# Interleaving the heads on TensorE: the recurrent scan, the first half's attention scores, and attention values on two column halves

## Chip, cores and metric

One core of a Trainium2 chip. The metric is the device time of one execution in microseconds (us); the time of a kernel is the median of its runs. Engines: PE (TensorE, matrix products), DVE (VectorE), ACT (ScalarE), POOL (GpSimd), SP (SyncE, which here only issues DMA transfers). PE's products are written to PSUM, from which DVE and ACT read.

## What is computed

One encoder layer over 1024 tokens of width 1024, in float32. A projection `x @ W_in` feeds two branches, which are merged; two layer norms and a product-key mixture of experts (PEER) follow. What matters here are the two branches.

```python
# branch A: forgetting attention, 8 heads of 64, causal, 128-query blocks
s = einsum('bhqd,bhkd->bhqk', q, k) * scale + c[q] - c[k]     # c: cumulative log forget gate
p = softmax(where(causal, s, -inf))
out = einsum('bhqk,bhkd->bhqd', p, v)

# branch B: RWKV-7, 8 heads of 64, a state of 64x64 per head
def frame_step(state, inp):
    sa = einsum('bhij,bhj->bhi', state, -kk_t)
    state = state * w_t + sa[..., None] * (kk_t * a_t) + v_t[..., None] * k_t
    return state, einsum('bhij,bhj->bhi', state, r_t)
...
x = LayerNorm(alpha * x + (sig(gA) * (yA @ P_A) + sig(gB) * (yB @ P_B)) @ W_o)
x = LayerNorm(alpha * x + PEER(x))     # 8 heads, top 16 of 16384 experts per token
```

## The kernel before

**Stages.** The tokens go in two halves of 512. Each half runs `fox` (branch A), `rwkv_half` (branch B), `merge_half` and `queries` (the expert scores). Then a dense block computes the experts of token tiles 5 to 7 over all 16384 experts, while the experts of tiles 0 to 4 are gathered row by row.

**Order of the work.** PE's order in the halves is the order in which the program is written; DVE, ACT and POOL get their queues from the framework's planner. Two things are woven into PE's order. A `Filler` holds projections of the next step; `F.fill(us)` issues as many of them as make up so much estimated time (`fill` in `fox`, `wait(WT[..])` in `rwkv_half`). A `Background` holds the top-k selection and the gathered experts (`topk`, `experts_in`): every `mm` and every transpose ticks it with the product's estimated time, and it issues its next piece when it has credit. The background has something to do only once the first half's expert scores exist, so in the second half and the dense block. It is mostly DVE work (top-k, and a reduction of 128x1024 for each gathered set of rows) and gathers on POOL's DMA queue. All this counts matmuls by their shapes, not by their time on the chip.

**Attention (`fox`).** The loop goes over `ct`, four pairs of heads; head `e` of a pair has its 64 features on partitions 64e to 64e+63 (`r`). For each block of 128 queries (`qi`) the scores against up to 512 keys are five products into the tile `S`: three with the high and low parts of q and k (`qh kh`, `qh kl`, `ql kh`, 64 rows of the array), one that adds the forget bias (`csel`, `ck`, 128 rows) and, on the last block of keys, the causal mask. In the first half (`joint`, four key tiles) both heads of a pair share one `S` tile of two banks, head 1 from column 512 on; in the second half the heads go one after the other. DVE takes the row maximum (`nm`), ACT the exponential (`pr`). The probabilities are transposed and multiplied with the values in `chunks`, a generator in the list `tail` that is advanced by `step` between later score blocks: per key block `kb` it transposes into `pt`, copies on ACT to `th`, and `pv` multiplies the 64 value columns `vc` with `th` into `po`, rows `r` of the output. `pv` runs one key block behind. At the end ACT copies `po` to `yu`, and after the second head `yu` is scaled by the reciprocal row sums and stored. The constant `PV32` is (1,1), so the branch with split values, and its DRAM tensor `vd`, is never taken.

**Scan (`unit` in `rwkv_half`).** Each pair of heads has eight chunks of 64 tokens. After the intra-chunk products (`M`, the triangular levels, `W_`, `At`, `Q`) a loop over the chunks carries the state `sigma`: per chunk and head two products make the next state (`BK` with `AV` over 128 rows, `At` with the state over the head's 64 rows), a copy by DVE (even chunks) or ACT (odd chunks) puts it into SBUF, and two products give the output (`AV` with `M`, the state with `Q`). Each head writes its own 64 partitions of the same PSUM tiles. A float32 product is two records in the trace.

Of the kernel before, what the change touches and what calls it, by code (L numbers as in the profile page):

```python
# [10 lines left out]
F32 = mybir.dt.float32  # L11
F32R = mybir.dt.float32r
# [8 lines left out]
T = 1024  # L21
# [31 lines left out]
SBUFS = 2  # L53
ORD, YTX = 1, 1
LNA = 1
PV32 = (1,1)
SM = 45
MANUAL = {mybir.EngineType.PE}
ALL = {mybir.EngineType.PE, mybir.EngineType.Pool, mybir.EngineType.DVE}
# [305 lines left out]
def body(ctx, g):  # L365
# [13 lines left out]

    g.yfd = dram("yfd", (512, T))  # L380
    g.kd = dram("kd", (4, 2, 128, T))
    g.vd = dram("vd", (T, 1024))
    g.vfd = dram("vfd", (T, 512))
    g.bvd = dram("bvd", (512, T))
    g.gtd = [dram(f"gtd{p}", (16, 128, n)) for p, (_, n) in enumerate(PARTS)]
# [125 lines left out]
def fox(g, hf, X):  # L511
# [2 lines left out]
    t0, n = g.t0, g.n  # L514
    nq, nb, ntt = n // 128, t0 // 128, (t0 + n) // 128
    joint = ntt <= 4
    f32 = PV32[hf]
    ck = g.ck
    cols = g.cols
    with ExitStack() as fx:  # L520
# [30 lines left out]
        with tc.tile_pool(name="fg", bufs=1) as fg, tc.tile_pool(name="xr", bufs=2) as xr:  # L551

            z = fg.tile([8, n], F32, name="z")
            ps = psA.tile([128, n], F32, name="pj")
            run(proj_gen(g, ps, FOX_F, X, 0))
            act.activation(z, ps[0:8, :], AF.Identity, bias=g.vec[0:8, V_FB:V_FB + 1])
            na = fg.tile([8, n], F32, name="na")
            dve.scalar_tensor_tensor(na, z, -1.0, z, op0=OP.mult, op1=OP.min)
            e = fg.tile([8, n], F32, name="fe")
            act.activation(e, na, AF.Exp)  # L560
            u = na
            dve.tensor_scalar(u, e, 1.0, None, op0=OP.add)
            lu = fg.tile([8, n], F32, name="flu")
            act.activation(lu, u, AF.Ln)
            dve.scalar_tensor_tensor(u, u, -1.0, e, op0=OP.add, op1=OP.subtract)
            dve.tensor_sub(lu, lu, u)
            dve.scalar_tensor_tensor(lu, z, 0.0, lu, op0=OP.min, op1=OP.subtract)
            dve.memset(e, 1.0)
            cc = z
            dve.tensor_tensor_scan(cc, e, lu, g.ccar, op0=OP.mult, op1=OP.add)  # L570
            dve.tensor_copy(g.ccar, cc[:, n - 1:n])
            act.activation(ck[0:8, cols], cc, AF.Copy, scale=-1.0)
            dve.scalar_tensor_tensor(ck[32:40, cols], cc, -1.0, ck[0:8, cols].bitcast(F32), op0=OP.mult, op1=OP.subtract)
            if "c" in g.dbg:
                sp.dma_start(g.dbg["c"][:, cols], cc)
            vw = fg.tile([128, 2, 4, 1024], F32R, name="vw")
            for c in range(4):
                raw = xr.tile([128, 1024], F32, name="xraw")
                sp.dma_start(raw, A["w"][FOX_V + c])
                split(g, vw[:, 0, c, :], vw[:, 1, c, :], raw, pool if c % 2 else dve)  # L580
            raw = xr.tile([128, 1024], F32, name="xraw")
            sp.dma_start(raw, A["foxtab"][:, 0:1024])
            act.copy(csel, raw.rearrange("p (a b) -> p a b", a=8))
            raw = xr.tile([128, 1024], F32, name="xraw")
            sp.dma_start(raw[:, 0:128], A["foxtab"][:, 1024:1152])
            act.copy(caus, raw[:, 0:128])
            act.copy(identr, ident)
            run(qk(0, psA))

            for tt in range(nq):  # L590
                ps = psA.tile([128, 512], F32, name="pj")
                t = slice(tt * 128, (tt + 1) * 128)
                for k in range(8):
                    s = slice(k * 128, (k + 1) * 128)
                    mm3(g, ps, X[0][:, k, t], X[1][:, k, t], vw[:, 0, :, s], vw[:, 1, :, s], k == 0, k == 7)
                rows_ = slice(t0 + tt * 128, t0 + (tt + 1) * 128)
                if any(PV32[hf:]):
                    vf = xr.tile([128, 512], F32, name="vf")
                    act.copy(vf, ps)
                    act.dma_start(g.vfd[rows_, :], vf)  # L600
                if all(PV32[hf:]):
                    continue
                vhl = xr.tile([128, 8, 2, 64], F32R, name="vhl")
                split(g, vhl[:, :, 0, :], vhl[:, :, 1, :], ps.rearrange("p (h d) -> p h d", h=8))
                act.dma_start(g.vd[rows_, :], vhl.rearrange("p h a d -> p (h a d)").bitcast(F32))
        fg2.close()
        vp = fx.enter_context(tc.tile_pool(name="vp", bufs=1))
        psS = fx.enter_context(tc.tile_pool(name="psS", bufs=2, space=PSUM))
# [16 lines left out]
        def chunks(ct, e, P_, yu, su, vc):  # L625
# [2 lines left out]
            pend = []  # L628
            r, x = (slice(0, 64), slice(64, 128)) if e == 0 else (slice(64, 128), slice(0, 64))

            def pv(kb, o, th, tl):
                vv = vc[:, kb, :]
                if f32:
                    mm(g, po[r, o:], vv, th[:, o:], kb == 0, kb == ntt - 1)
                    return
                mm(g, po[:, o:], vv, th[:, o:], kb == 0, False)
                mm(g, po[:, o:], vv, tl[:, o:], False, kb == ntt - 1)

            for kb in range(ntt):
                q0 = max(0, kb - nb)  # L640
                pt = psT.tile([128, n], F32, name="pt")
                for qi in range(q0, nq):
                    pe.transpose(pt[:, qi * 128:(qi + 1) * 128], P_[qi][:, kb * 128:(kb + 1) * 128], ident)
                    g.B.tick(0.11)
                o = q0 * 128
                th = sm.tile([128, n], F32 if f32 else F32R, name="th")
                tl = None
                if f32:
                    act.copy(th[:, o:], pt[:, o:])
                else:  # L650
                    tl = sm.tile([128, n], F32R, name="tl")
                    split(g, th[:, o:], tl[:, o:], pt[:, o:])
                pend.append((kb, o, th, tl))
                if len(pend) > 1:
                    pv(*pend.pop(0))
                yield
            for p_ in pend:
                pv(*p_)
            if f32:
                act.copy(yu[r, :], po[r, :])  # L660
            else:
                yt = sm.tile([128, n], F32, name="yt", bufs=1)
                act.copy(yt[r, :], po[x, :])
                dve.tensor_add(yu[r, :], po[r, :], yt[r, :])
            yield
            if e:
                dve.reciprocal(su, su)
# [13 lines left out]
        for ct in range(4):  # L681
# [1 line left out]
            (qh, ql), (kh, kl) = qkt["q", ct], qkt["k", ct]  # L683
            vcs = []
            for h in (2 * ct, 2 * ct + 1):
                if f32:
                    vc = vp.tile([128, ntt, 64], F32, name="vc", bufs=24 // ntt)
                    sp.dma_start(vc, g.vfd[0:ntt * 128, h * 64:(h + 1) * 64].rearrange("(t p) c -> p t c", p=128))
                    vcs.append(vc)
                    continue  # L690
                vc = vp.tile([128, ntt, 128], F32R, name="vc", bufs=24 // ntt)
                sp.dma_start(vc.bitcast(F32), g.vd[0:ntt * 128, h * 128:(h + 1) * 128].rearrange("(t p) c -> p t c", p=128))
                vcs.append(vc)
            if ct < 3:
                F.add(qk(ct + 1, psJ), f"qk{ct + 1}")
# [2 lines left out]
            for es in ((0, 1),) if joint else ((0,), (1,)):  # L698
                P_ = {e: [] for e in es}
                for qi in range(nq):  # L700
                    q = slice(qi * 128, (qi + 1) * 128)
                    nk = (nb + qi + 1) * 128
                    ps = psS.tile([128, T], F32, name="S")
                    for e in es:
                        h = 2 * ct + e
                        r = slice(64 * e, 64 * e + 64)
                        base = 512 * e if joint else 0
                        for b0 in range(0, nk, 512):
                            b1 = min(nk, b0 + 512)
                            ks = slice(b0, b1)  # L710
                            o = ps[:, base + b0:base + b1]
                            mm(g, o, qh[r, q], kh[r, ks], True, False)
                            mm(g, o, qh[r, q], kl[r, ks], False, False)
                            mm(g, o, ql[r, q], kh[r, ks], False, False)
                            last = b1 == nk
                            mm(g, o, csel[:, h, :], ck[:, ks], False, not last)
                            if last:
                                mm(g, ps[:, base + nk - 128:base + nk], identr, caus, False, True)
                            step(1)
                            F.fill(fill)  # L720
# [20 lines left out]
def rwkv_half(g, hf, X, kt):  # L741
# [12 lines left out]
    with ExitStack() as fx:  # L754
# [164 lines left out]
        def unit(ct):  # L919
# [101 lines left out]
            for c in range(NC):  # L1021
                par = c % 2
                pss = psS.tile([128, 64], F32, name="s")
                for e in range(2):
                    r = rows[e]
                    mm(g, pss[r, :], BK[:, e, c, :], AV[:, e, c, :], True, False)
                    mm(g, pss[r, :], At[r, c, :], g.sigma[r, ct, par, :], False, True)
                (act.copy if c % 2 or SM & 64 else dve.tensor_copy)(g.sigma[:, ct, 1 - par, :], pss)
                for e in range(2):
                    r = rows[e]  # L1030
                    mm(g, py[r, c, :], AV[:, e, c, :], M[:, e, c, 0:64], True, False)
                    mm(g, py[r, c, :], g.sigma[r, ct, par, :], Q[r, c, :], False, True)
                wait(WT[7])
            act.copy(yr[:, ct, :], fl(py))
# [806 lines left out]
```

## Time and profile before

| | |
|---|---|
| time, median of 3 runs (lowest, highest) | 3988.88 us (3987.24, 3991.28) |
| the profiled execution, its time and its span | 3954.7 us, 3952.9 us |
| busy share of the span: PE, DVE, ACT, POOL | 85%, 58%, 31%, 59% |
| mean granted clock of TensorE | 0.897 |
| attention of the first half, of the second half | 62 to 201 us, 890 to 1130 us |
| recurrent branch of the first half, of the second half | 201 to 640 us, 1130 to 1690 us |
| dense loop | from 2530 us to the end |

A row of the timeline has the start and the length in us, the engine, the line of the kernel, the operation, the written and the read tile, the rows and columns of the array, the shape of the moving data, and the number of records merged into it. Most products have line 263, that of the helper `mm`, so the tile's name tells them apart. A merged row's length reaches from the first start to the last modelled end, and the ends of pipelined products overlap; the cost of a product is read from the distance between starts. In the scan's rows `Tm` is the buffer that holds `At`, `x` the one that holds `Q`, and `s` stands for both PSUM tiles (`pss` and `py`).

### The profile page before, as it was taken

The numbers are of one execution on the slowest core, as the hardware profiler recorded it, in microseconds if no ns is written. First come the engines' busy times: TensorE is split into PE (matmuls) and PEld (weight loads), VectorE is DVE, ScalarE is ACT, GpSimd is POOL, SyncE is SP. The second block draws the span as 40 slices with busy tenths as digits, with TensorE's granted clock in tenths as the row PEclk, the third lists the DMA queues.
The fourth block names the chain that finished last, engine by engine and source line by source line (L and its number), as shares of the span: only waits on it lengthen the run. The fifth ranks groups of instructions, "written<-read, shape, count | busy, mean of one in ns | idle before, by whom it ended". The sixth has DMA issues, their size and how long they took to land. (4 is left out here: it accounts for less than half of the span.)

```text
span 3952.9 us, 55417 instructions
## 1 busy us (share of the span) xinstructions
PE 3367.2 (85%) x20656; PEld 2429.7 (61%) x20656; DVE 2310.8 (58%) x4773; ACT 1243.7 (31%) x2522; POOL 2341.8 (59%) x1848
## 2 busy tenths in 40 slices
PE   7999999989987877877837676699998899999998
PEld 5577676775555655656713333477776677776676
DVE  3133423448889887899637576366665576733334
ACT  3342212333333111122214343233333333333333
POOL 2031114435666546667647667688887788777872
PEclk9898898998988777888968778799999899999999
DMA  4121114447777666877768789999998999999993
GB/s 134 43 91 36 36 63 138 168 150 243 259 256 260 213 213 223 292 252 262 278 250 269 263 289 301 322 362 367 375 349 319 374 377 387 376 367 406 403 407 128
DMA packets 376575, 1018.03 MB, mean 258 GB/s; under 512 B 108273, under 2 KB 124913, under 8 KB 376049
## 3 DMA queue, kind: packets, MB, share of 16 engines
q0 software_dynamic: 184320, 671.17, 46.5%
q1 hardware_dynamic: 179872, 322.54, 23.9%
q10 hardware_dynamic: 12112, 20.78, 1.4%
q8 instruction: 162, 2.65, 0.3%
q14 instruction: 109, 0.88, 0.1%
HBM read 960.03 MB, written 54.33 MB: 257 GB/s over the span
## 5 line engine op out<-in xcount | busy, mean ns | idle before, releaser
L1398 POOL DMA_INDIRECT g<-u,eidx x640 | 779.0, 1217 | 436.5 <-DVE hh L1403 154.6
L1403 DVE CUSTOM_DVE_ANT_0 g<-g,ext 128x1024 f32<-128x1024 f32 x640 | 879.5, 1382 | 230.3 <-DMA g<-u,eidx 228.7
L281 POOL TENSOR_TENSOR wl<-wraw,wh 128x1024 fp32r<-128x1024 f32 x131 | 322.9, 2465 | 562.4 <-ACT wh L280 513.1
L1675 POOL DMA_INDIRECT vr<-v,ve x454 | 488.6, 1076 | 130.3 <-issue 104.1
L263 PE MATMUL pg<-vr,win 128*32 128x512 f32 x1816 | 307.8, 645 | 115.6 <-DMA vr<-v,ve 115.3
L263 PE MATMUL b<-xh,uh 128*128 128x384 f32 x1024 | 353.7, 345 | 52.2 <-DVE C L1561 29.6
L263 PE MATMUL b<-xh,ul 128*128 128x384 f32 x1024 | 357.4, 349 | 19.1 <-POOL ul L281 19.1
L263 PE MATMUL b<-xl,uh 128*128 128x384 f32 x1024 | 351.9, 344 | 0.0
L263 PE MATMUL v<-vl,ch 128*128 128x512 f32 x768 | 310.1, 404 | 22.7 <-POOL vl L281 22.6
L263 PE MATMUL pj<-xh,wh 128*128 128x512 f32 x624 | 292.0, 468 | 22.3 <-DVE ql L546 8.5
L280 ACT CAST wh<-wraw 128x1024 fp32r<-128x1024 f32 x150 | 157.2, 1048 | 486.3 <-PE pj L263 264.3
L263 PE MATMUL v<-vh,cl 128*128 128x512 f32 x768 | 305.3, 398 | 0.0
L263 PE MATMUL v<-vh,ch 128*128 128x512 f32 x768 | 304.7, 397 | 0.0
L280 ACT CAST uh<-uraw 128x512 fp32r<-128x512 f32 x256 | 158.7, 620 | 399.4 <-PE b L263 359.0
L263 PE MATMUL pj<-xh,wl 128*128 128x512 f32 x624 | 262.0, 420 | 6.4 <-POOL wl L281 3.7
L263 PE MATMUL pj<-xl,wh 128*128 128x512 f32 x624 | 263.9, 423 | 1.9 <-DVE xl L281 1.9
L1675 POOL DMA_INDIRECT C<-v,ve x186 | 196.6, 1057 | 105.3 <-issue 39.4
L263 PEld LDWEIGHTS b<-xh,uh 128*128 128x128 f32 x1024 | 196.7, 192 | 66.5 <-DVE C L1561 34.3
L263 PEld LDWEIGHTS b<-xh,ul 128*128 128x128 f32 x1024 | 196.6, 192 | 56.6 <-issue 32.7
L281 POOL TENSOR_TENSOR ul<-uraw,uh 128x512 fp32r<-128x512 f32 x128 | 170.6, 1333 | 92.8 <-ACT uh L280 66.7
L281 DVE TENSOR_TENSOR vl<-vraw,vh 128x512 fp32r<-128x512 f32 x128 | 122.8, 960 | 171.4 <-ACT vh L280 164.7
L263 PEld LDWEIGHTS pg<-vr,win 128*32 128x32 f32 x1816 | 52.3, 112 | 275.2 <-DMA vr<-v,ve 191.4
(352 smaller groups left out, 6897.9 us busy)
## 6 DMA issues: line engine op xcount, KB each, us to landing
wraw<-w SPq DMA_DIRECT2D x150, 512.0 KB, 3.5
uraw<-ut SPq DMA_DIRECT2D x128, 512.0 KB, 6.9
vraw<-vt SPq DMA_DIRECT2D x128, 512.0 KB, 6.7
cd<-S SPq DMA_DIRECT2D x30, 512.0 KB, 15.6
C<-cd SPq DMA_DIRECT2D x80, 192.0 KB, 6.1
g<-u,eidx POOLq DMA_INDIRECT x640, 6.1
gtd<-tmp ACTq DMA_DIRECT2D x32, 256.0 KB, 3.1
g<-gtd SPq DMA_DIRECT2D x32, 256.0 KB, 3.3
```

The source lines that it names most:

```text
L263: g.pe.matmul(o, l, r, start=start, stop=stop_)
L280: g.act.copy(hi, src)
L281: (lo_eng or g.dve).tensor_sub(lo, src, hi.bitcast(F32))
L1398: pool.indirect_dma_start(out=gg, out_offset=None, in_=A["u"], in_offset=bass.IndirectOffsetOnAxis(ap=idx[:, s_:s_ + 1], axis=0))
L1403: dve.tensor_tensor_reduce(out=gg, in0=gg, in1=xt, scale=1.0, scalar=0.0, op0=OP.mult, op1=OP.add, accum_out=hh[:, k:k + 1])
L1675: g.pool.indirect_dma_start(out=place, out_offset=None, in_=g.A["v"], in_offset=bass.IndirectOffsetOnAxis(ap=self.meta[i][1][:, t:t + 1], ...
```

## The change

Three edits, and the removal of the unused branch.

1. In the scan the two heads' products of one kind stand next to each other: both `BK`-`AV`, then both `At`-`sigma`, the copy, both `AV`-`M`, both `sigma`-`Q`.
2. In the first half's scores the two heads alternate within each of the three q-k products; the bias and mask products, with the tail steps and the filling, follow head by head.
3. The values go by two key blocks: the even block writes the rows of `po` that belong to the head (`r`), the odd block the other 64 rows (`x`). `pv` runs two to three blocks behind (`th` has four buffers). At the end ACT copies the other half to `yt`, and DVE adds the halves into `yu`; in the first half the first 128 queries have no odd block, and ACT copies them.

```diff
-            def pv(kb, o, th, tl):
-                vv = vc[:, kb, :]
-                if f32:
-                    mm(g, po[r, o:], vv, th[:, o:], kb == 0, kb == ntt - 1)
-                    return
...
+            def pv(two):
+
+                for kb, o, th in two:
+                    mm(g, po[x if kb % 2 else r, o:], vc[:, kb, :], th[:, o:], kb < 2, kb >= ntt - 2)
...
+                th = sm.tile([128, n], F32, name="th", bufs=4)
+                act.copy(th[:, o:], pt[:, o:])
+                pend.append((kb, o, th))
+                if len(pend) > 2 and kb % 2 == 0:
+                    pv(pend[:2])
+                    del pend[:2]
                 yield
-            for p_ in pend:
-                pv(*p_)
-            if f32:
-                act.copy(yu[r, :], po[r, :])
...
+            pv(pend)
+            o = max(0, 1 - nb) * 128
+            yt = sm.tile([128, n], F32, name="yt", bufs=1)
+            act.copy(yt[r, o:], po[x, o:])
+            if o:
+                act.copy(yu[r, 0:o], po[r, 0:o])
+            dve.tensor_add(yu[r, o:], po[r, o:], yt[r, o:])
             yield
...
-                    for e in es:
-                        h = 2 * ct + e
-                        r = slice(64 * e, 64 * e + 64)
-                        base = 512 * e if joint else 0
-                        for b0 in range(0, nk, 512):
-                            b1 = min(nk, b0 + 512)
-                            ks = slice(b0, b1)
-                            o = ps[:, base + b0:base + b1]
-                            mm(g, o, qh[r, q], kh[r, ks], True, False)
-                            mm(g, o, qh[r, q], kl[r, ks], False, False)
-                            mm(g, o, ql[r, q], kh[r, ks], False, False)
+                    for b0 in range(0, nk, 512):
+                        b1 = min(nk, b0 + 512)
+                        ks = slice(b0, b1)
+
+                        for a, k, first in ((qh, kh, True), (qh, kl, False), (ql, kh, False)):
+                            for e in es:
+                                r = slice(64 * e, 64 * e + 64)
+                                mm(g, ps[:, 512 * e * joint + b0:512 * e * joint + b1], a[r, q], k[r, ks], first, False)
+                        for e in es:
+                            base = 512 * e * joint
                             last = b1 == nk
-                            mm(g, o, csel[:, h, :], ck[:, ks], False, not last)
+                            mm(g, ps[:, base + b0:base + b1], csel[:, 2 * ct + e, :], ck[:, ks], False, not last)
                             if last:
                                 mm(g, ps[:, base + nk - 128:base + nk], identr, caus, False, True)
                             step(1)
                             F.fill(fill)
...
                 pss = psS.tile([128, 64], F32, name="s")
-                for e in range(2):
-                    r = rows[e]
+
+                for e, r in enumerate(rows):
                     mm(g, pss[r, :], BK[:, e, c, :], AV[:, e, c, :], True, False)
+                for r in rows:
                     mm(g, pss[r, :], At[r, c, :], g.sigma[r, ct, par, :], False, True)
                 (act.copy if c % 2 or SM & 64 else dve.tensor_copy)(g.sigma[:, ct, 1 - par, :], pss)
-                for e in range(2):
-                    r = rows[e]
+                for e, r in enumerate(rows):
                     mm(g, py[r, c, :], AV[:, e, c, :], M[:, e, c, 0:64], True, False)
+                for r in rows:
                     mm(g, py[r, c, :], g.sigma[r, ct, par, :], Q[r, c, :], False, True)
```

More of the change, by code (lines that the diff above doesn't have):

```diff
@@ L55 @@
 LNA = 1
-PV32 = (1,1)
 SM = 45
@@ L381, in body @@
     g.kd = dram("kd", (4, 2, 128, T))
-    g.vd = dram("vd", (T, 1024))
     g.vfd = dram("vfd", (T, 512))
@@ L516, in fox @@
     joint = ntt <= 4
-    f32 = PV32[hf]
     ck = g.ck
@@ L596, in fox @@
                 rows_ = slice(t0 + tt * 128, t0 + (tt + 1) * 128)
[L597 to L605, printed above, removed]
+                vf = xr.tile([128, 512], F32, name="vf")
+                act.copy(vf, ps)
+                act.dma_start(g.vfd[rows_, :], vf)
         fg2.close()
@@ L629, in chunks @@
             r, x = (slice(0, 64), slice(64, 128)) if e == 0 else (slice(64, 128), slice(0, 64))
-            def pv(kb, o, th, tl):
-                vv = vc[:, kb, :]
-                if f32:
-                    mm(g, po[r, o:], vv, th[:, o:], kb == 0, kb == ntt - 1)
-                    return
-                mm(g, po[:, o:], vv, th[:, o:], kb == 0, False)
-                mm(g, po[:, o:], vv, tl[:, o:], False, kb == ntt - 1)
+            def pv(two):
+                for kb, o, th in two:
+                    mm(g, po[x if kb % 2 else r, o:], vc[:, kb, :], th[:, o:], kb < 2, kb >= ntt - 2)
             for kb in range(ntt):
@@ L645, in chunks @@
                 o = q0 * 128
-                th = sm.tile([128, n], F32 if f32 else F32R, name="th")
-                tl = None
-                if f32:
[L649 to L655, printed above, removed]
-                yield
-            for p_ in pend:
-                pv(*p_)
-            if f32:
-                act.copy(yu[r, :], po[r, :])
[L661 to L664, printed above, removed]
+                th = sm.tile([128, n], F32, name="th", bufs=4)
[4 more added lines that the diff above has]
+                    del pend[:2]
+                yield
+            pv(pend)
[5 more added lines that the diff above has]
+            dve.tensor_add(yu[r, o:], po[r, o:], yt[r, o:])
             yield
@@ L685, in fox @@
             for h in (2 * ct, 2 * ct + 1):
[L686 to L692, printed above, removed]
+                vc = vp.tile([128, ntt, 64], F32, name="vc", bufs=24 // ntt)
+                sp.dma_start(vc, g.vfd[0:ntt * 128, h * 64:(h + 1) * 64].rearrange("(t p) c -> p t c", p=128))
                 vcs.append(vc)
```

## The prediction, written before the result was known

> **What bounds the kernel now.** I read the timeline by stages first (busy time of each engine in each stretch), since the page's average of 85% on PE mixes stages with different limits, then the timeline of the changed places, then the groups by tile. Columns: stretch, its length, then busy time and instructions of PE, PEld, DVE, ACT, POOL, then the granted clock, the DMA share and GB/s.
>
> ```profile
> core 0: us, PE busy (x) PEld busy (x) DVE busy (x) ACT busy (x) POOL busy (x), PEclk, DMA share, GB/s
> 62.00:201.30 139.30, 124.23 (x473) 73.87 (x472) 21.34 (x30) 48.31 (x122) 12.31 (x6) 0.89 0.17 51
> 890.00:1130.50 240.50, 226.33 (x839) 120.57 (x837) 191.46 (x503) 89.43 (x163) 130.28 (x99) 0.93 0.75 245
> 1130.50:1316.00 185.50, 145.53 (x1156) 113.11 (x1155) 169.10 (x348) 59.58 (x86) 131.55 (x92) 0.87 0.76 258
> 1316.00:1690.00 374.00, 302.61 (x3001) 224.83 (x3001) 297.86 (x722) 70.77 (x113) 211.66 (x162) 0.77 0.71 237
> 1690.00:2000.00 310.00, 229.93 (x999) 181.69 (x999) 259.64 (x543) 77.95 (x112) 205.11 (x134) 0.88 0.74 253
> 2530.00:3953.00 1423.00, 1326.44 (x7046) 1027.39 (x7046) 771.99 (x1072) 483.90 (x1004) 1082.58 (x908) 0.97 0.93 356
> ```
>
> The attention of the first half (62 to 201) is PE's: 124 of 139 us, DVE at 15%. The attention of the second half (890 to 1130) is PE's too, but DVE, which there also does the background work (top-k and the gathered experts), is at 80%. From 1130 to 2000 PE and DVE take turns: PE idles 40 + 71 + 80 = 191 us there, mostly on DVE. The dense block (from 2530) is PE's and is not touched: its start moves with the end of the second half. The eight scans (four pairs of heads, two halves) lie inside the stretches before 640 and between 1314 and 1680. The first of the first half and all four of the second, same columns:
>
> ```profile
> 344.10:367.10 23.00, 23.00 (x138) 16.32 (x137) 1.50 (x6) 2.39 (x6) 2.34 (x1) 0.76 0.11 36
> 587.60:611.30 23.70, 23.70 (x148) 16.67 (x147) 2.60 (x6) 2.39 (x6) 0.66 (x1) 0.87 0.33 111
> 1314.70:1345.00 30.30, 27.80 (x138) 19.17 (x138) 14.40 (x53) 2.39 (x6) 12.86 (x11) 0.62 0.60 202
> 1425.00:1457.90 32.90, 28.54 (x140) 19.71 (x139) 18.86 (x46) 4.48 (x8) 14.86 (x13) 0.59 0.63 205
> 1541.00:1575.30 34.30, 28.37 (x140) 19.69 (x139) 17.03 (x44) 2.39 (x6) 16.09 (x12) 0.59 0.64 213
> 1653.00:1679.60 26.60, 25.15 (x148) 17.53 (x147) 18.04 (x54) 2.39 (x6) 15.41 (x13) 0.82 0.84 287
> ```
>
> (The fourth of the first half stands second.) In the first half a scan is nothing but PE: 100% busy, DVE 1.5 to 2.6 us of 23. Of the 138 matmul records of a scan 128 are its own: eight chunks, eight products each, two records a product.
>
> **The scan.** One chunk at full clock, and two products at the low clock:
>
> ```profile
> 344.19 0.33 PE L263 MATMUL s<-AV,BK 128*64 128x64 f32 x2
> 344.45 0.33 PE L263 MATMUL s<-sigma,Tm 64*64 64x64 f32 x2
> ...
> 344.96 0.33 PE L263 MATMUL s<-sigma,Tm 64*64 64x64 f32 x2
> ...
> 345.99 0.33 PE L263 MATMUL s<-x,sigma 64*64 64x64 f32 x2
> 346.24 0.50 PE L263 MATMUL pj<-xh,wh 128*128 128x512 f32 x1
> ```
> ```profile
> 366.36 0.47 PE L263 MATMUL s<-M,AV 128*64 128x64 f32 x2
> 366.76 0.47 PE L263 MATMUL s<-x,sigma 64*64 64x64 f32 x2
> ```
>
> Each product starts 0.256 us after the one before (2.05 us for eight), 0.40 at the low clock: they run strictly one after another, though the two heads use different halves of the array. The change puts the heads' equal products next to each other. What such neighbours cost, the trace shows in three other places:
>
> ```profile
> 341.29 1.15 PE L263 MATMUL s<-BK,x 64*64 64x64 f32 x32
> 342.27 1.10 PE L263 MATMUL s<-M,x 64*64 64x64 f32 x32
> ```
> ```profile
> 287.35 1.16 PE L263 MATMUL pm<-arv,bk 64*128 64x128 f32 x16
> 288.44 0.70 PE L263 MATMUL s<-ag,tab 128*128 128x512 f32 x1
> ```
> ```profile
> 3862.44 1.07 PE L263 MATMUL pg<-C,win 128*32 128x512 f32 x8
> 3863.33 1.04 PE L263 MATMUL pg<-vr,win 128*32 128x512 f32 x8
> ```
>
> Sixteen 64x64 products with the heads alternating take 0.98 us, 0.123 a pair. Eight products that alternate between the two halves of the rows take 1.09 us, 0.14 each, where each has twice the columns of a scan product. Four products on four strips of columns, 512 columns each, take 0.89 us together. So both kinds of neighbours that the change makes (row halves with column halves, and column halves over all rows) do overlap. What a pair costs when its neighbour pairs have another shape isn't shown. It lies between 0.26 (the second head free) and 0.256 + 0.123 = 0.38 (the second follows the first); I take 0.26, since the four strips show three of four free. A chunk is then four pairs, 1.04 us for 2.05, and 1.6 for 3.2 at the low clock.
>
> First half: of its 23.0 + 23.4 + 23.8 + 23.7 = 94 us of scan (the second and third lie like the first), projections take three times 9 and once 19 records of some 0.24 with two shape changes, 12 to 13 us; 81 remain and half of it is 40. The stretch without projections, in which the clock falls, gets shorter, worth some 2 more: **42 us**. The chain through the state does not take over: its copy starts 0.36 after the state's product (344.96) and ends 0.58 after,
>
> ```profile
> 345.32 0.22 DVE L1028 COPY sigma<-s 128x64 f32<-128x64 f32 x1 [0.62 <-PE s L263]
> ```
>
> while three pairs, 0.78 us, lie between the product and the next that needs it.
>
> Second half: the same edit, but DVE has 14.4 to 18.9 us of work in each scan. A scan of 30.3, 32.9, 34.3, 26.6 loses half of some 23 us of products, but can't get below its DVE time plus the 1 or 2 us at the start where PE waits: I put the four at 18, 20, 20, 19, which saves 12 + 13 + 14 + 7.5, some 46, and take **40**, because every second state copy is on DVE and may stand behind a background reduction of 1.38 us:
>
> ```profile
> L1403 DVE CUSTOM_DVE_ANT_0 g<-g,ext 128x1024 f32<-128x1024 f32 x640 | 879.5, 1382 | 230.3 <-DMA g<-u,eidx 228.7
> ```
>
> Sixteen such copies, each late by at most 1.2 us after the slack of 0.2: 0 to 19 us. Ends for this part: 20 (40 less all of that) and 59 (92 us of products become 32 chunks of 1.04, 33 us, all at full clock).
>
> **The first half's scores.** Three products of one head for the narrowest and the widest block:
>
> ```profile
> 65.71 0.32 PE L263 MATMUL S<-kh,qh 64*128 64x128 f32 x1
> 66.19 0.33 PE L263 MATMUL S<-ck,csel 128*128 128x128 f32 x1
> 81.88 0.50 PE L263 MATMUL S<-kh,qh 64*128 64x512 f32 x1
> 82.76 0.50 PE L263 MATMUL S<-ck,csel 128*128 128x512 f32 x1
> ```
>
> 0.48 and 0.88 us, so 0.68 on average over the four widths. Afterwards the second head's three run on the other 64 rows beside the first's, into another bank, as the 64*128 rows above do. Saved: one head's three in 16 query blocks, 16 x 0.68 = 11 us. The order of the rest (bias, causal mask, filling) stays. The second half has one head at a time here, so its instructions come in the old order.
>
> **The values.** Now each key block is a product with 64 columns of weights, one at a time; afterwards an even block goes to one column half and an odd block to the other, and the halves are added.
>
> ```profile
> 95.16 1.07 PE L263 MATMUL po<-th,vc 128*64 128x512 f32 x2
> 96.16 0.50 PE L263 MATMUL pj<-xh,wh 128*128 128x512 f32 x1
> ```
> ```profile
> 62.00:210.00 148.00, 23.76 (x64) 6.22 (x64) 4.64 (x8) 0.90 0.16 50
> 890.00:1131.00 241.00, 59.92 (x128) 12.43 (x128) 4.63 (x8) 0.93 0.75 245
> ```
>
> (The last two rows are those of this tile alone: PE, PEld, ACT.) One 512-wide product takes 1.00 us; four on four strips took 0.89. A pair therefore costs its wider member. Per head the first half streams 512 + 384 + 256 + 128 = 1280 columns, afterwards 512 + 256 = 768: 23.8 us become 14.3, 9.5 saved. The second half streams 5 x 512 + 384 + 256 + 128 = 3328, afterwards 3 x 512 + 256 = 1792: 59.9 become 32.3, 27.6 saved.
>
> One rule of the Trainium skill speaks against this and against half of the scan's pairs: "TensorE: Matmul & The Clock Gate", Part 3 (The mechanism), says that a weight load overlaps matmuls in flight only where its row group differs, and all pairs of column halves have the same rows. The strips (3862.44) have the same 128 rows, and eight records in 0.89 us contradict it; by the rule the sum would be that of the second rival below.
>
> What is added: 16 DVE additions where there were none, priced by the nearest row,
>
> ```profile
> L676 DVE TENSOR_TENSOR yu<-yu,pt x4: 675/686/686, 987.5 to 1130.6; 128x512 f32<-128x512 f32 x4
> ```
>
> 0.69 us each; the old ACT copy is replaced by one of the same size, and eight short ones come in the first half. In the first half DVE is free. In the second, 5.5 us more come to DVE, which has 49 us idle in that stretch: nothing, or 5.5 if that is gone. The result's bank is now freed by DVE, so up to 1.4 us later; the next head's first pair comes three steps later, a third of a query block each (240.5 / 32 / 3 = 2.5 us), so 7.5 us cover it. Without the cover: 8 x 1.4 = 11 us. No transfer is added or moved, on no queue: the old buffer of split values was never written, since the constant took the other branch.
>
> First half: (11 + 9.5) x 0.9 = **19 us** (a tenth lost at the waits for the next projection, which shorter scores cover less). Second half: 27.6 on PE, but DVE would go from 80% to 197 of 213, 92%, so I count two thirds: **18 us**, between 0 and 28.
>
> **Sum.** 42 + 40 + 19 + 18 = 119 us. The background is issued by counts of matmuls, which stay the same, so none of it falls out of the second half into the dense block. The profiled execution took 3954.7 us (span 3952.9), 34 us below the median of the runs: 3954.7 - 119 = 3836 for it, and 3988.9 - 119 = **3870** for the median.
>
> **Rivals.** *Second half absorbed by DVE* (chance 0.13): DVE's 169 + 298 + 260 us of 870 from 1130 on, and its 80% before, turn PE's gain into waits of PE. For it: PE already waits 191 us there. Against: in the scans DVE has 14 to 19 us of 27 to 34. Then only 42 + 19 = 61 remain: 3928. *Column halves don't overlap* (0.10): their pairs cost 0.38 rather than 0.26, a chunk saves 0.76 rather than 1.0, scans 32 + 30, values 3 (only shape changes), scores 10: 75, so 3914. *The pairs change nothing* (0.04), if the queue still runs them singly: 3989. *Slower* (0.07): only PE's order is written by hand; the order on DVE is planned from estimated times. A new PE order can put the background ahead of the masks and sums of the units, which PE waits for between 1130 and 2000. It decides from the point where PE's 191 idle us grow by 127 (two thirds), so that gain and 8 us more are gone; grown by 150 it gives 4020. Nothing in the rows shows such growth. *More* (0.06): the scans stay at full clock (33 us for 81 and for 92) and DVE never binds: 48 + 59 + 20 + 28 = 155, so 3834.
>
> **Numbers.** The forecast has 0.60, its own range 3845 to 3895. The range over the cases goes from the best one to the DVE rival, 3834 to 3930. A difference of 0.2% (8 us) is about what a measurement can tell from none. Faster 0.60 + 0.13 + 0.10 + 0.06 = 0.89, same 0.04, slower 0.07.
>
> **What would show it.** Scan: records of two heads starting within a few ns, four starts per chunk 0.26 apart, and first-half scans of some 12 to 13 us in place of 23 (0.38 apart would speak for the second rival). Scores: the two heads' starts together. Values: the tile's PE time near 14 and 32 us. If first-half stages shrink by 61 but the stretch 890 to 1690 by far less than 58, DVE took it. I am wrong if PE's idle time between 1130 and 2000 grows by over 40 us, or if the dense block gets longer.

## The result and the profile after

| | before | after |
|---|---|---|
| time, median of six runs (lowest to highest) | 3985.46 us (3973.53 to 3991.28) | 3838.49 us (3820.99 to 3847.03) |
| the profiled execution and its span | 3954.7, 3952.9 | 3838.68, 3836.9 |
| mean granted clock in it | 0.897 | 0.900 |

The ratio is 0.9628 [0.9604, 0.9653]: 147 us, or 3.7%, faster. The two profiled executions are only 116 us apart, as the one of before was at the fast end of its runs; the last part comes back to that.

First the timeline by stages of the kernel before, cut at marks that both kernels have: the attention of the first half, its recurrent branch up to the last scan's end, (the next stage, up to the second attention, is left out, 290 us in both), the second attention, the second branch up to the first scan, its four scans with what lies between, and the merge up to the expert scores. Columns as in the prediction.

```profile
62.70:200.90 138.20, 123.79 (x472) 73.87 (x472) 21.34 (x30) 47.72 (x121) 12.31 (x6) 0.89 0.17 52
200.90:611.10 410.20, 393.71 (x4118) 301.66 (x4116) 144.68 (x223) 106.93 (x172) 80.88 (x43) 0.91 0.17 58
...
901.40:1130.10 228.70, 215.17 (x792) 112.26 (x792) 180.83 (x468) 83.14 (x155) 130.28 (x99) 0.93 0.78 255
1130.10:1316.50 186.40, 145.93 (x1157) 113.11 (x1155) 169.60 (x351) 59.58 (x86) 132.01 (x93) 0.87 0.76 258
1316.50:1679.40 362.90, 292.87 (x2961) 218.94 (x2961) 290.27 (x701) 64.32 (x103) 206.49 (x158) 0.77 0.71 238
1679.40:2063.80 384.40, 257.72 (x1137) 191.90 (x1136) 292.25 (x661) 97.36 (x152) 248.36 (x176) 0.83 0.75 260
```

The same stages of the kernel after, and the dense block as the last row:

```profile
64.10:178.20 114.10, 98.43 (x471) 64.17 (x472) 25.88 (x38) 48.70 (x129) 12.32 (x6) 0.90 0.20 63
178.20:534.20 356.00, 338.57 (x4118) 263.18 (x4116) 144.62 (x223) 107.04 (x172) 80.97 (x43) 0.98 0.19 65
...
824.10:1035.10 211.00, 198.54 (x792) 112.93 (x792) 178.19 (x464) 82.53 (x154) 119.47 (x94) 0.87 0.79 260
1035.10:1228.90 193.80, 152.50 (x1161) 117.76 (x1159) 181.18 (x360) 60.89 (x87) 140.66 (x97) 0.86 0.78 265
1228.90:1565.20 336.30, 255.67 (x2959) 192.71 (x2959) 298.18 (x706) 64.63 (x103) 203.58 (x157) 0.78 0.75 256
1565.20:1956.30 391.10, 270.80 (x1139) 201.97 (x1137) 292.26 (x665) 97.14 (x152) 255.13 (x178) 0.80 0.75 259
...
2421.30:3837.00 1415.70, 1318.54 (x7046) 1019.98 (x7046) 782.56 (x1072) 483.30 (x1004) 1085.16 (x908) 0.97 0.94 358
```

The lengths changed by -24, -54, -18, +7, -27, +7 and (dense) -7 us. The first half gave 78 us. The second half gave 44 in its attention and scans, and 14 came back before the first scan and in the merge. In its scans DVE's busy time hardly moved (290 to 298 us), while the stage shrank by 27: DVE's share went from 80% to 89%. These are the lengths of one execution of each kernel; e4 shows how far a stage scatters.

The scans themselves in the kernel after: the first and fourth of the first half, and all four of the second, same columns.

```profile
321.30:332.40 11.10, 11.10 (x140) 7.91 (x139) 1.50 (x6) 2.40 (x6) 2.36 (x1) 1.00 0.21 72
...
520.80:534.30 13.50, 13.50 (x148) 9.38 (x147) 2.70 (x6) 2.40 (x6) 0.67 (x1) 1.00 0.46 152
1227.60:1246.40 18.80, 14.21 (x138) 9.59 (x137) 15.32 (x48) 2.40 (x6) 11.14 (x10) 0.81 0.81 289
1328.70:1350.20 21.50, 14.60 (x138) 9.89 (x138) 18.79 (x43) 4.49 (x8) 12.56 (x11) 0.72 0.82 273
1432.70:1458.30 25.60, 17.36 (x138) 11.73 (x137) 17.72 (x47) 2.40 (x6) 15.36 (x13) 0.59 0.86 298
1542.30:1565.30 23.00, 20.63 (x147) 13.52 (x146) 16.80 (x51) 2.39 (x6) 14.14 (x11) 0.59 0.81 292
```

In the first half a scan is still nothing but PE, and takes 11 us for 23, at the full clock where the first had 0.76 (the fourth, with more projections in it, 13.5 for 23.7). In the second half each takes 3 to 8 us more than DVE's time in it (18.8 for 15.3, 25.6 for 17.7). One chunk of the first scan, and the start of the projections behind it, from the timeline of PE:

```profile
321.39 0.34 PE L262 MATMUL s<-AV,BK 128*64 128x64 f32 x4
321.65 0.33 PE L262 MATMUL s<-sigma,Tm 64*64 64x64 f32 x4
321.92 0.34 PE L262 MATMUL s<-M,AV 128*64 128x64 f32 x4
322.18 0.33 PE L262 MATMUL s<-x,sigma 64*64 64x64 f32 x4
322.44 0.50 PE L262 MATMUL pj<-xh,wh 128*128 128x512 f32 x1
```

Each row is now four records, both heads' product, and the rows start 0.262 us apart: a pair costs what a single product did (0.256).

### The profile page after: what moved, and what is told of

It reads as the page before. It is cut to its first block, busy times and chain, and to the rows that moved or that the text cites. A ratio compares the mean times of both kernels' runs of the same rounds, so it can differ in the third digit from the quotient of the medians.

```text
span 3836.9 us, 55419 instructions
## 1 busy us (share of the span) xinstructions
PE 3244.6 (85%) x20656; PEld 2364.6 (62%) x20656; DVE 2339.6 (61%) x4789; ACT 1246.1 (32%) x2530; POOL 2343.9 (61%) x1848
## 5 line engine op out<-in xcount | busy, mean ns | idle before, releaser
L262 PE MATMUL b<-xh,uh 128*128 128x384 f32 x1024 | 351.5, 343 | 48.5 <-DVE C L1539 28.0
L279 ACT CAST vh<-vraw 128x512 fp32r<-128x512 f32 x256 | 157.7, 621 | 183.2 <-PE v L262 124.5
```

The lines of the kernel that those rows point to most:

```text
L262: g.pe.matmul(o, l, r, start=start, stop=stop_)
L279: g.act.copy(hi, src)
```

## The experiments

**The parts one at a time (e1, e2, e3), and the kernel before once more (e4).** Each of the first three is the kernel before with one of the three edits of the diff.

```diff
 e1: before + edit 1 (the loop over the chunks in the scan)
 e2: before + edit 2 (the first half's scores)
 e3: before + edit 3 (pv, th, yt and the addition)
 e4: before, unchanged
```

> The kernel before with the scan's edit alone. Theory (the edits act where PE is the bound, and add up): the four scans of the first half take 11 us each instead of 23, the first half's recurrent branch goes from 410 to about 356 us, the second half's from 363 to about 336, because its scans wait for DVE and the gathered rows; in all 75 to 100 us faster. Rival 1 (DVE absorbs the second half altogether): 54 us faster and no more. Rival 2 (pairing over column halves does not overlap): four starts per chunk 0.26 and 0.38 apart and first-half scans of 14 to 15 us.

Measured: 3872.28 us, ratio 0.9727 [0.9688, 0.9765]; the kernel before took 3976.94 beside it, so the scan alone saves 105 us, a little over the 75 to 100 expected. Its stages, the first branch and then the second branch up to the first scan, and the four scans:

```profile
202.90:558.00 355.10, 337.12 (x4116) 261.38 (x4114) 144.36 (x223) 106.82 (x172) 80.89 (x43) 0.98 0.19 65
...
1073.50:1268.30 194.80, 151.84 (x1159) 117.67 (x1157) 170.17 (x351) 59.89 (x86) 135.38 (x94) 0.86 0.74 249
1268.30:1596.20 327.90, 247.80 (x2955) 187.75 (x2955) 294.80 (x699) 64.20 (x103) 200.09 (x154) 0.80 0.77 260
```

The whole gain of the first branch (355 for 410) is the scan's. In the second half the scans' stage is 35 us shorter than in the kernel before (327.9 for 362.9), which rules out that DVE takes up the second half's gain altogether. The stage before it is 8 us longer, but it is 6 us longer in e2 too, where nothing of the second half was changed.

> The kernel before with the edit of the first half's scores alone. Theory: 11 us faster, all of it in the attention of the first half (138 to about 127 us), nothing elsewhere. Rival: the shorter scores only uncover waits for DVE's maximum, ACT's exponential and the next projection, and the stage stays within 3 us of 138.

Measured: 3960.82 us, ratio 0.9952 [0.9932, 0.9973]: 16 us. The first attention took 123.8 us for 138.2 (135.1 in e4), so the rival, that it stays within 3 us, is out.

> The kernel before with the values' edit alone. Theory: 10 us faster in the first half's attention and 18 in the second's (229 to 211), 28 in all. Rival: the second half's gain comes back in the recurrent branch that follows, because DVE and the gathers were already behind; then 10 us in all, and the stretch between the second half's attention and its first scan is longer by what the attention won.

Measured: 3945.98 us, ratio 0.9899 [0.9859, 0.994]: 31 us. The values' own PE time, first half and second half (this tile alone: PE, PEld, DVE, ACT):

```profile
62.00:210.00 148.00, 16.66 (x64) 4.53 (x64) 4.44 (x8) 5.86 (x16) 0.84 0.16 50
890.00:1131.00 241.00, 35.30 (x128) 7.82 (x128) 5.51 (x8) 4.64 (x8) 0.94 0.80 266
```

23.8 and 59.9 before, so most of the forecast saving is there (59.9 to 35.3, where a pair at the price of its wider member would give 32.3). The first attention as a whole was only 3 us shorter, 135.3 for 138.2, where 10 were expected; its granted clock was 0.84 for 0.89. The second attention took 199.0 us for 228.7 in this execution, but the branch behind it 576 for 549. That branch took 564 and 562 us in e2 and e4, whose second half is the old one, so about half of these 26 us is scatter. As its granted clock in the scans was also lower (0.74 for 0.77), how much of the rest is the branch taking back what the attention gave, and how much the clock, this run does not tell.

> The kernel before once more, unchanged, profiled again. Its first profiled execution took 3954.7 us while its timed runs took 3973.5 to 3991.3. Theory (that execution happened to be fast): this one takes some 3985 us, and the 30 us more lie in one or two stages of the second half or the dense block. Rival (a profiled execution is faster than a timed one): again about 3955 us. Against itself the ratio is 1.000.

Measured: 3984.89 us, ratio 1.0012 [0.999, 1.0033], from 3959.31 to 3998.84 over ten runs; the profiled one was its fastest. So an unchanged kernel scatters by 14 to 26 us around its median, and a single profile cannot carry a difference of 20 us. The profiled time, 3959 us, is the one that the rival named (again about 3955), not the theory's 3985. A general rule that a profiled execution is the faster one isn't shown: in e1, e2, e9 and e10 it was the fastest of its runs, in e3, e6 and e11 the slowest. For this kernel it stays open. The stage of the four scans in e4, and then in e2, whose second half is the old one as well:

```profile
1317.30:1690.70 373.40, 299.27 (x2962) 224.10 (x2962) 293.13 (x701) 64.37 (x103) 202.37 (x157) 0.76 0.69 231
1305.20:1676.00 370.80, 299.99 (x2962) 225.18 (x2962) 291.14 (x701) 64.38 (x103) 201.84 (x157) 0.76 0.69 232
```

That is 8 to 10 us more than the 362.9 of the first profile. The other stages of the old second half lie closer together: 226 to 230 us for the attention, 186 to 193 up to the first scan, 384 for the merge; the first branch took 410 or 411 in all three. The medians of e1 to e3 add up: 105 + 16 + 31 = 152 for the 147 of the whole change.

**What a pair costs (e5).** The kernel after with the output's first pair moved up, so that equal shapes follow each other:

```diff
                 for e, r in enumerate(rows):
                     mm(g, pss[r, :], BK[:, e, c, :], AV[:, e, c, :], True, False)
+                for e, r in enumerate(rows):
+                    mm(g, py[r, c, :], AV[:, e, c, :], M[:, e, c, 0:64], True, False)
                 for r in rows:
                     mm(g, pss[r, :], At[r, c, :], g.sigma[r, ct, par, :], False, True)
                 (act.copy if c % 2 or SM & 64 else dve.tensor_copy)(g.sigma[:, ct, 1 - par, :], pss)
-                for e, r in enumerate(rows):
-                    mm(g, py[r, c, :], AV[:, e, c, :], M[:, e, c, 0:64], True, False)
```

> The changed kernel with the scan's four pairs in another order: the two pairs over 128 rows (next state's and output's first products) stand next to each other, then the two pairs over 64 rows, so that the array changes its tiling twice per chunk instead of four times. Theory (most of a lone pair's 0.26 us is the change of shape, since pairs of one shape follow each other every 0.123): a chunk without projections takes 2 x (0.26 + 0.12) = 0.77 us instead of 1.05, unless the chain through the state (0.36 to the copy, 0.22 copy, 0.06 back) sets some 0.8; first-half scans 9 us instead of 11, in all 8 to 15 us faster. Rival (the 0.26 is the latency of a product whose neighbour needs the same strip of the array, whatever its shape): no change, within 3 us.

Measured: 3813.18 us, ratio 0.9598 [0.9571, 0.9625], 158 us from the kernel before (3971.37) where the kernel after had 147; the two intervals overlap a little, so the proof is in the scan's rows. One chunk of the first scan, and the first row of the next:

```profile
330.56 0.34 PE L262 MATMUL s<-AV,BK 128*64 128x64 f32 x4
330.73 0.29 PE L262 MATMUL s<-M,AV 128*64 128x64 f32 x4
330.94 0.33 PE L262 MATMUL s<-sigma,Tm 64*64 64x64 f32 x4
331.11 0.28 PE L262 MATMUL s<-x,sigma 64*64 64x64 f32 x4
331.32 0.34 PE L262 MATMUL s<-AV,BK 128*64 128x64 f32 x4
```

A chunk takes 0.76 us for 1.05 with the same products: two changes between 128 and 64 rows fewer, 0.15 us each. (The records inside the rows show it too: behind the last product of 128 rows, which starts at 330.79, the next load starts at 330.94; within one shape the products follow each other every 0.06.) The first-half scans, from the first product's start to the last one's end, fell from 11.0 to 8.7 us and the first branch from 356.0 to 346.1 us, about four times these 2.3.

**Do DVE's state copies hold up the second half (e6)?** All copies of the state to ACT:

```diff
-SM = 45
+SM = 109
```

> The changed kernel with all state copies of the scan on ACT; before, every second one is on DVE. Theory (the second half's scans lose their time at their start, where PE waits for DVE's At and Q, and not at the state copies): within 5 us of the changed kernel. Rival (the term of the prediction: state copies stand behind background reductions on DVE): second-half scans of 88 us in all lose 10 us or more, and the kernel is 8 to 15 us faster.

Measured: 3823.75 us, ratio 0.9624 [0.9599, 0.9648], no difference from the kernel after (0.9628), and its second half's scans take 90 us in all for 89. The copies cost nothing that can be measured.

**Is it DVE's background that bounds the second half's scans (e7, e8)?** The rate turns a product's time into credit for the background, for attention, branch and merge in turn.

```diff
-RATEP = (1, 1, 0.9)
+RATEP = (1, 0.8, 0.9)   # e7
+RATEP = (1, 0, 0.9)     # e8
```

> The changed kernel with the background issued at 0.8 of its rate in the recurrent branches. Theory (with the scans shorter, the second half's recurrent branch is set by DVE and the gathers that the background puts there): that branch gets 20 to 50 us shorter and what comes after it longer by about as much; total within 15 us. Rival (PE's own products and its clock set the branch): the branch stays within 10 us, and the kernel gets slower by the 20 to 40 us of background that is left for later.

Measured: 3863.29 us, ratio 0.9736 [0.971, 0.9761], some 43 us slower than the kernel after by the ratios' difference (0.0108 of 3971), so the expected tie is out. Its stage of the four scans:

```profile
1220.50:1495.30 274.80, 232.44 (x2960) 176.16 (x2960) 247.31 (x526) 61.02 (x100) 160.85 (x123) 0.85 0.74 246
```

DVE has 51 us less to do (247 for 298) and the stage is 62 us shorter (275 for 336), with DVE at 90%. So DVE's work weighs heavily there, PE being at 85%. It isn't the only limit: e5, with a faster scan and DVE's work as before (297 us), has that stage at 318. And the work returns later with more on top: merge 464 us for 391, scores 509 for 465. Taking the background out of the branch does not pay.

> The changed kernel with no background at all issued in the recurrent branches; it all comes later. Only the second half's recurrent branch is of interest, not the total. Theory: without background its scans take the 11 to 13 us of the first half's, 46 in all instead of 88, and the branch some 370 us instead of 530, as the first half's 356 us. Rival (something else differs in the second half, the clock for one): scans stay above 17 us each.

Measured: 4082.81 us, a single execution. This was a miss as an experiment: at rate 0 the scans' stage was 268 us, much as the 275 at 0.8, and the reductions still ran in it (103 of them; 105 at 0.8, 134 in the kernel after), while what follows grew to 518 (merge) and 782 us (scores). The four scans took 18 to 26 us each, not the 11 to 13 expected, so scans without DVE's background were not seen. Why the branch still held them is open; that the planner puts instructions issued later into DVE's earlier gaps would fit, and was not tried.

**The other way: more background where PE got faster (e9, e10), and more gathers in flight (e11).** All three with e5's order.

```diff
-RATEP = (1, 1, 0.9)
+RATEP = (1, 1.15, 0.9)      # e9
+RATEP = (1.15, 1.0, 1.0)    # e10
-LEAD = 3
+LEAD = 4                    # e11
```

> The kernel of the two-shapes order with the background issued at 1.15 of its rate in the recurrent branches. Theory (DVE is the bound of the second half's branch, and its time follows the number of background pieces issued there; at 0.8 the branch was 55 to 60 us shorter, DVE 47 us less busy in it, and the rest 87 us longer): the branch gets 25 to 45 us longer, the rest 35 to 60 us shorter, in all 5 to 20 us faster than the two-shapes kernel. Rival (at 1.0 the branch has no room left, so that every piece costs there as much as it saves later): within 5 us, or slower.

Measured: 3839.26 us, ratio 0.964 [0.9615, 0.9665] (e5: 0.9598), no faster than e5, as the rival had it. The branch grew by 45 us (210.0 + 350.6 for 197.4 + 317.9) for 29 more reductions, and the merge shrank by 21 for 29 fewer.

> The kernel of the two-shapes order with the background's rate at 1.15 in the attention and at 1.0 instead of 0.9 in the merge; 1.0 in the recurrent branch as before. Theory (the second half's attention is PE's bound and DVE has some 30 us idle there): the attention grows by less than 10 us while 10 to 15 more pieces go there, and the later stages lose 20 us or more; in all 8 to 20 us faster than the two-shapes kernel. Rival (with the values paired, DVE is the attention's bound as well): it grows by what is saved later, within 5 us.

Measured: 3834.67 us, ratio 0.9632 [0.9606, 0.9658]. Again no faster than e5. The attention grew by 36 us for 16 more reductions, 2.2 us each, and the merge gave back 10 for 15 fewer. Both agree with e7 from the other side: in these profiles a piece of background costs 1.6 to 2.2 us where it is added, and the merge gives back 0.7 for each that leaves it.

> The kernel of the two-shapes order with the gathers of background rows issued four reductions ahead instead of three (five buffers as before). Theory (DVE is bound by its own work in the second half's branch, 89% busy; its waits for rows are 9 us there): within 5 us. Rival (late rows hold DVE and with it PE, above all at the start of the scans): DVE's waits for rows fall from 9 to under 3 us in the branch, which gets 10 us or more shorter.

Measured: 3802.83 us, ratio 0.9547 [0.952, 0.9574], the fastest version: 182 us from the kernel before (3984.68). Its interval touches that of e5, 0.9571 to 0.9625. DVE's waits for gathered rows in the scans' stage are 11.4 us, and e5 has 15.0:

```profile
DVE g L1381 <- DMA g<-u,eidx: 11.4, 15, 1.6
```

But that stage is not shorter in its profile (324 us for 318), and its runs had a granted clock of 0.910 for e5's 0.907. Where its gain lies is open.

## Why the prediction was right, point by point

**The total** (3870 forecast, within 3834 to 3930) came out 31 us below the forecast. On the profiled executions the sum was nearly exact, 119 for 116, but that is luck, as errors in both directions cancelled: the first half gave 17 us more than its 61, the second half 28 less than its 58 (18 - 7 in the attention and the stage behind it, 27 - 7 in the scans and the merge, together 30 after rounding), and the dense block and the scores 8 that were not in the sum.

**The scan is the term that was mis-sized.** It stood at 82 us and measured 105 alone (e1, by medians). What was too low is the first half's part; the second half's depends on which execution of the old kernel it is compared with.

*First half, 42 predicted, 54 measured.* The halving was right: two heads' records start together and a pair costs 0.26, so the lower bound that I took holds. The four scans went from 94 to 47 us, 47 for the 42. What failed is the "some 2 more" for the clock. Take the start of the stretch behind the first scan, before and after:

```profile
367.10:373.10 6.00, 6.00 (x25) 4.28 (x24) 1.98 (x3) 0.58 (x1) 0.00 (x0) 0.50 0.04 17
```
```profile
332.40:351.00 18.60, 18.60 (x206) 14.28 (x207) 8.34 (x11) 4.42 (x8) 2.40 (x1) 1.00 0.13 44
```

PE is 100% busy in both, but the old kernel has half the clock for the first 6 us behind the scan (and 1.00 from 373.1 on), where the new one has all of it: the low clock of the old scan reached into the work behind it. Half of 6 us is 3, and the stretch up to the next scan did go from 59.7 to 56.8 us. At the full clock scan and stretch both gain, 5 us more in the scans and, over the three stretches between them, 7 behind them. The row with the low clock inside the scan stood in the prediction, but I priced its products alone and not what comes after.

*Second half, 40 predicted, 27 measured in the scans' stage of the two profiles, 19 with the stage before it.* Against the 371 and 373 us that the same old stage took in e2 and e4 the 336 are a gain of 34 to 37, so how far the 40 was missed is open by 10 us. The mechanism was named (a scan cannot get below its DVE time), and the waits on top of it were put too low. I put the scans at 18, 20, 20, 19; they took 18.8, 21.5, 25.6, 23.0 in the rows above, in all 89 for 124: 35 us saved where the working had 46. What there was to win stood in DVE's waits. Before and after, over the scans' stage (columns: total us, times, longest):

```profile
DVE sigma L1028 <- PE s L263: 47.4, 11, 7.1
```
```profile
DVE sigma L1006 <- PE s L262: 14.5, 7, 3.5
```

DVE stood 47 us at the state copy, waiting for PE (49 in e4, 48.5 in e2), and 33 of them are gone. By the stage's rows all of DVE's idle time fell by 34.5 us (362.9 - 290.3 = 72.6, and 336.3 - 298.2 = 38.1); 8 went into more DVE work, and the other 27 are what came off the stage. PE, on the other side, waits a little more: for `x` and `Tm` (`Q` and `At` among them) 67.6 us became 72.4. The first view is before, the second after:

```profile
PE s L263 <- DVE x L961: 33.0, 15, 5.9
PE s L263 <- DVE Tm L971: 20.3, 7, 7.3
PE s L263 <- DVE x L1018: 7.5, 4, 3.2
PE s L263 <- DVE Tm L1012: 6.8, 3, 2.7
```
```profile
PE s L262 <- DVE x L938: 35.7, 15, 4.2
PE s L262 <- DVE Tm L948: 18.2, 4, 7.3
PE s L262 <- DVE x L995: 11.7, 4, 4.9
PE s L262 <- DVE Tm L989: 6.8, 3, 3.4
...
PE s L262 <- DVE sigma L1006: 3.6, 3, 1.8
```

The timeline of all engines shows the worst place, at the third scan:

```profile
1435.03 1.23 DVE L1381 CUSTOM_DVE_ANT_0 g<-g,ext 128x1024 f32<-128x1024 f32 x1 [1.73 <-DMA g<-u,eidx]
...
1436.19 0.46 DVE L989 SCALAR_TENSOR_TENSOR Tm<-tab,dgc,s 128x64 f32<-128x64 f32 x2
...
1436.52 0.33 PE L262 MATMUL s<-sigma,Tm 64*64 64x64 f32 x4 [3.35 <-DVE Tm L989]
...
1441.26 0.69 DVE L995 TENSOR_TENSOR x<-s,arv 128x512 f32<-128x512 f32 x1
...
1442.00 0.48 PE L262 MATMUL s<-x,sigma 64*64 64x64 f32 x4 [4.89 <-DVE x L995]
```

PE stands 3.35 us for `At` and 4.89 for `Q`: DVE does background reductions ahead of both, and two of them wait for gathered rows themselves. This is the wait that the "1 or 2 us at the start" of a scan left out. The dispute over the copies (0 to 19 us) ends near 0: PE waits 3.6 us for them in all (`sigma` above), and e6 moves nothing. The third and fourth scan also kept a clock of 0.59, so "all at full clock", the good end, did not come.

**The attention of the first half**: 19 predicted, 24 measured. On PE the scores' tile `S` gave 12.0 (11 predicted) and the values' tile 9.3 (9.5 predicted). The rows are the busy time of one tile, `S` before, then `S` and the values after:

```profile
62.00:210.00 148.00, 40.85 (x160) 26.74 (x160) 13.19 (x16) 18.26 (x64) 0.90 0.16 50
```
```profile
64.00:186.00 122.00, 28.90 (x160) 20.66 (x160) 13.20 (x16) 18.28 (x64) 0.90 0.19 61
...
64.00:186.00 122.00, 14.45 (x64) 4.08 (x64) 4.44 (x8) 5.89 (x16) 0.90 0.19 61
824.00:1036.00 212.00, 37.58 (x128) 7.93 (x128) 5.50 (x8) 4.64 (x8) 0.87 0.79 261
```

The tenth that I took off for waits was not lost: PE has 21.3 us less to do, and the stage is about 22 shorter (over the profiles at hand 135 to 139 us with the old code, 114 to 118 with the new). The 24 of the two profiles is the upper end of that.

**The attention of the second half**: 18 predicted, 17.7 measured. The values took 37.6 us where I had 32.3; at a higher clock they took 35.3 (e3's row: 0.94 for 0.87). DVE rose from 79% to 84% of the stage and not to 92%, since the stage shrank less. That the size fits so well is luck: the seven other profiles with this attention at the same rate (e3, e5 to e9, e11) have 199 to 210 us, the four with the old one 226 to 230, so the gain is rather 22 on the mean. The two thirds that I counted were too few. The stage behind it was 7 us longer in the kernel after (193.8), but with the old attention it took 186 to 195 (the last in e1), so it isn't shown that it took back part of this gain.

**The rivals.** "Column halves don't overlap" and "the pairs change nothing" are out by 321.39: two heads in one row of four records, 0.26 apart. So the rule of the Trainium skill ("TensorE: Matmul & The Clock Gate", Part 3 (The mechanism)), that a load overlaps only products of another row group, does not hold for these pairs, whose weights lie on the same 128 rows: the second head's load starts some 5 ns after the first head's product. "Absorbed by DVE" got its due in part: 30 of 58 us were kept by the two profiles, 41 and 45 against the same stages of e2 and e4, not none. For "slower" PE's idle time had to grow by 127 us. Over the three stages from the second attention's end to the end of the merge it went from 237 to 242 us (186.4 - 145.9 and so on), far from the 40 at which I would have been wrong; the dense block did not get longer (1416 us; 1418 to 1423 in the profiles with the old second half), and the background did not fall into it: 245 reductions run there before and after.

**147 against 116.** Over 49 timed executions of the kernel before (e4's ten and those beside the experiments), from 3956.7 to 3998.8 us, time falls by 26 us for each 0.01 of granted clock (correlation -0.68); over the six of the kernel after by 24 (-0.88). The profiled execution of before had 0.897 with a typical 0.894, that of after 0.900 with a typical 0.904: by these slopes, an estimate, 8 us each, which makes 132 of the 116. The other 15 us stay open; the old profile's short stage of scans (363 us for the 371 and 373 of e2 and e4) is a place where 8 to 10 of them would fit. I had carried the profile's sum over to the median unchanged.

## What to carry to other kernels

Where products use only half of the array, put the products that use the other half right next to them, and products of one shape next to each other: the first made two cost what one did, the second took a further quarter off the chunk. Before sizing such a gain in a stage that two engines share, read how long the other engine waits for the one made faster (here 47 us): that is about what there is to win, and the rest becomes a wait in the other direction. The faster scan of e5 took 45 us off that stage and left 5 us of this wait. Price a low granted clock for what follows it, too, and don't rest a difference of 20 us on one profile.

## What was not expected of the hardware

- The granted clock in the first-half scans rose from 0.72 to 0.87 in the four to 1.00 in all, with PE 100% busy before and after: the same products, two at a time, in half the time. The clock also stayed up behind the first scan (1.00 where it was 0.50 for 6 us). Over whole executions e1, with the scan alone, had a median clock of 0.910 where the kernel before had 0.894. That the pairs cause it is shown by e1; what in them the throttle answers to is not.
- The change between a product over 128 rows and one over 64 costs 0.15 us in the scan (a chunk of 1.05 us with four changes, 0.76 with two), more than half of what a pair takes.
- A kernel that is not changed runs between 3957 and 3999 us, and the slower executions tend to be those with the lower granted clock (correlation -0.68).
